# Three edits in the order of a hybrid encoder layer: the norm's VectorE steps bound to their written place, the splits of the heads' output spread over more of the GLU stage, and channel sums ten taps later

## Chip, cores and metric

The kernel runs on one core of one Trainium2 chip. The metric is the device time of one execution in microseconds. Three runs of the kernel before took 2465.12, 2465.72 and 2464.33 us, median 2465.12 us. The engines are called as the profile calls them: PE (TensorE, matmuls) and PEld (its weight loads), DVE (VectorE), ACT (ScalarE), POOL (GpSimd), SP (SyncE, which here only issues DMAs).

## The reference, cut to what matters

One layer for a sequence of 512 frames with 2048 channels, in float32:

```python
h = rmsnorm(x, g_pre)
qkv, z_a, b_raw, a_raw, glu_in, z_b, gate_logits = split(h @ w_in)
# A: gated DeltaNet, 16 heads of 128
o_a = gated_delta_chunked(q, k, v, g_log, beta)
o_a = rmsnorm(o_a, g_dn_out) * silu(z_a)
y_a = o_a @ w_br_a
# B: Conformer convolution
u = glu(glu_in)
u = causal_depthwise_conv(u, w_dw) + b_dw          # 31 taps
u = silu(layernorm(u, ln_g, ln_b)) * silu(z_b)     # over the 2048 channels
y_b = u @ w_br_b
mixed = (gate_a * y_a + gate_b * y_b) @ w_out
x = x + rmsnorm(mixed, g_post)
x = x + rmsnorm(sigmoid(x @ w_ple_gate) * (p @ w_ple_proj), g_ple)
```

The change touches the depthwise convolution, the layernorm and what turns `o_a` into operands of the product with `w_br_a`.

## The kernel before

**Products.** Channels or frames lie on the 128 partitions, tiles are 128x512 float32. Every product of two float32 matrices is made of three matmuls: each operand is split into a high part (a cast on ACT) and a low part (a subtraction on DVE or POOL), and high by high, high by low and low by high are added up in PSUM. Weights come in pieces: SP loads a raw tile of two pieces (L122), ACT casts the high part (L127), and DVE or POOL subtracts the low part (L128, by `low_part[0]`). A piece serves 12 matmuls. The ring of split pieces has four buffers (`ring`), so that one is in use and up to three stand ready.

**Stages.** After the input norm come the gate products with a Strassen-like scheme, then the heads (48 tiles of q, k, v and the chunked recurrence), then the GLU tiles, branch A (`o_a @ w_br_a`, L1076), branch B (`u @ w_br_b`, the same function), the output product and the embedding product. The part of this case runs from the GLU tiles to the start of branch B.

**GLU and convolution.** `glu_pair(i)` (L991) gives channel tile i: two tiles of 48 matmuls each, the first ends in a sigmoid on ACT (L911), the second in a product on DVE (L981). For i above 11 each pair is followed by one job of branch A of 48 matmuls (`next_ya`). `convs` (L938) does the 31 taps of a tile on DVE, one instruction for each tap (L954), bound to its written place; from the GLU stage on it reads a copy of the tile in PSUM (`up`). Two tiles are done beside it by `side_convs` (L964): ACT makes a product for a tap (L972) and POOL adds it (L973). A finished tile is written to DRAM (L961) and added to a running sum over channels on POOL by `filtered` (L915: L918 for the first tile, L920 for the others); for DVE's tiles this is called at tap 18 of the next tile. Tiles of the convolutions come from the pool `s2` with 17 buffers.

**Splits of the heads' output.** `split_oa` (L1064) takes the 16 heads' tiles one by one: ACT casts the high part (L1067), POOL subtracts the low part (L1069, bound). It is started after GLU pair 9 with a period of 15 ticks and finished by force after pair 11. The 32 tiles lie in the pool `lop` (23 buffers) and, from head 11's low part on, in `s2`.

**Norm.** `layer_norm` (L1134) loads the filtered tiles again as each is done (L1139, SP), takes the mean from a product of the channel sum with ones (L1143, L1145), subtracts it from each tile (L1150, DVE), squares the tile on ACT (L1152), and adds the squares up (L1154, DVE). Four small products give the variance (L1158), POOL takes the power -0.5 (L1162), a product with ones spreads it into PSUM (L1170). Then for each tile: multiply (L1174, DVE), SiLU (L1175, ACT), multiply with the other gate (L1179, DVE), high part (L1181, ACT), low part (L1183, DVE). These are the operands uT of branch B. Branch A has four column blocks j of 192 matmuls; at the end of a block four DVE instructions (L1102) empty its four PSUM banks, which the next block uses.

**What sets the order.** The code is written as generators. `tick` is called after every matmul of these stages and advances each active generator when its period, or the number that it yielded last, has run out: this gives the written order. Then a scheduler orders each engine's queue: it runs the program on a model of the engines and gives an engine, whenever that is free, the instruction that comes first in the written order among those that are ready, so that an instruction that is ready early moves ahead of earlier ones that are not. Buffers of a pool are given out in written order. `pin` (`keep_in_program_order`, L104) takes this freedom away on one side: the instruction is placed behind the one written last before it on the same engine. Later unbound instructions may still move ahead of it. On the chip each queue is then worked off in that order.

Of the kernel before, what the change touches and what calls it, by code (L numbers as in the profile page):

```python
# [12 lines left out]
ALU = mybir.AluOpType  # L13
# [68 lines left out]
def _body(ctx, tc, A, out):  # L82
    nc = tc.nc
# [20 lines left out]
    pin = tc.keep_in_program_order  # L104
# [4 lines left out]
    def vv(col, n=1):  # L109
        return vec[:, col:col + n]  # L110
# [28 lines left out]
    jobs = deque()  # L139
    active = []  # L140

    def spawn(gen, period, key=None):
        active.append([gen, period, period, key])
# [11 lines left out]
    def finish(key=None):  # L155
        while any(key is None or a[3] == key for a in active):
            for a in list(active):
                if (key is None or a[3] == key) and next(a[0], "end") == "end":
                    active.remove(a)
# [755 lines left out]
    def filtered(i, y):  # L915
        if not acc:
            acc.append(slots.tile([P, T], F32, tag="s", name="acc"))
            nc.gpsimd.tensor_copy(acc[0], y)  # L918
        else:
            nc.gpsimd.tensor_tensor(acc[0], acc[0], y, ALU.add)  # L920
        done.add(i)

    def near(held=True):
        if not waiting or len(taken) == NK:
            return None
        i, u = waiting.popleft()
        taken.add(i)
        if ups and held:
            up = ups.tile([P, T], F32, tag="u", name="up")
            nc.scalar.copy(up, u)  # L930
            u = up
        y = cpool[0].tile([P, T], F32, tag=cpool[1], name="uc")
        nc.scalar.activation(y, u, AF.Identity, scale=vv(V_DW + i * TAPS + TAPS - 1), bias=vv(V_BDW + i))
        return i, u, y

    def pace(s):
        return (3 + s % 2) if ups else CP

    def convs():
        ready = last = None  # L940
        while scanning[0] < NH // 2 - 1:
            yield 4
        while len(done) < NK:
            ready = ready or near()
            if not ready:
                if last and len(taken) == NK:
                    filtered(*last)
                    last = None
                yield 1
                continue  # L950
            (i, u, y), ready = ready, None
            w0 = V_DW + i * TAPS
            for s in range(1, TAPS):
                pin(nc.vector.scalar_tensor_tensor(y[:, s:], u[:, 0:T - s], vv(w0 + TAPS - 1 - s), y[:, s:], ALU.mult, ALU.add))  # L954
                if s == 18 and last:
                    filtered(*last)
                    last = None
                if s == 24:
                    ready = near()
                yield pace(s)  # L960
            nc.sync.dma_start(u_dram[i], y)  # L961
            last = i, y
# [28 lines left out]
    def glu_pair(i):  # L991
        glu_b(i)
        glu_a(i)
# [48 lines left out]
    gate_b = [[None] * 4 for _ in range(NTT)]  # L1042

    jobs.append(lambda: spawn(convs(), CP, "convs"))
    for i in range(2, 5):
        glu_pair(i)
# [13 lines left out]
    def low(n, name, dt=F32R):  # L1060
        return lop.tile([P, T], dt, tag="lop", name=name) if n < LOP else s2.tile([P, T], dt, tag="s2", name=name)
    oT = []

    def split_oa():  # L1064
        for h in range(NH):
            oh = low(2 * h, "oh")
            nc.scalar.copy(oh, o_a[h])  # L1067
            ol = low(2 * h + 1, "ol")
            pin(nc.gpsimd.tensor_tensor(ol, o_a[h], oh.bitcast(F32), ALU.subtract))  # L1069
            oT.append((oh, ol))  # L1070
            yield
# [39 lines left out]
    def next_ya():  # L1111
        j, q = ya.pop(0)
        if q == 1:
            jobs.append(lambda: load_gate(j))
        branch(A["w_br_a"], j, q, oT, evac_ya)

    for i in range(5, NK):
        glu_pair(i)
        if i == 9:
            jobs.append(lambda: spawn(split_oa(), 15, "oa"))  # L1120
        if i == 11:
            jobs.append(lambda: finish("oa"))
        if i > 11:
            next_ya()
# [6 lines left out]
    def hp(name):  # L1131
        return hpool.tile([P, T], F32, tag="h", name=name)

    def layer_norm():  # L1134
        for i in range(NK):
            while i not in done:
                yield
            u_t[i] = hp("ur")
            nc.sync.dma_start(u_t[i], u_dram[i])  # L1139
            yield 1  # L1140
        low_part[0] = nc.vector
        pm = ups.tile([P, T], F32, tag="u", name="sum_ps")
        mm(pm, ones, acc[0], start=True, stop=True)  # L1143
        mean = ups.tile([P, T], F32, tag="u", name="mean_ps")
        nc.scalar.activation(mean, pm, AF.Copy, scale=1.0 / D)  # L1145
        acc2 = hp("acc2")
        yield 6
        for i in range(NK):
            u = u_t[i]
            nc.vector.tensor_tensor(u, u, mean, ALU.subtract)  # L1150
            sq = hp("lsq") if i else acc2
            nc.scalar.activation(sq, u, AF.Square)  # L1152
            if i:
                nc.vector.tensor_tensor(acc2, acc2, sq, ALU.add)  # L1154
            yield 7
        pvr = ups.tile([P, T], F32, tag="u", name="var_ps")
        for tt in range(NTT):
            mm(pvr[:, tt:tt + 1], acc2[:, tt * P:(tt + 1) * P], ones[:, 0:1], start=True, stop=True)  # L1158
        var = lnp.tile([P, NTT], F32, name="var")
        nc.vector.tensor_scalar(var, pvr[:, 0:NTT], 1.0 / D, EPS, ALU.mult, ALU.add)  # L1160
        rst = lnp.tile([P, NTT], F32, name="rst")
        nc.gpsimd.tensor_tensor(rst, var, mhalf_c[:, 0:NTT], ALU.pow)  # L1162
        dg = hp("dg")
        for tt in range(NTT):
            nc.vector.tensor_scalar(dg[:, tt * P:(tt + 1) * P], ident, rst[:, tt:tt + 1], None, ALU.mult)
        for i in range(3):
            load_zb(i)
        yield 12
        rstd = ups.tile([P, T], F32, tag="u", name="rstd_ps")
        mm(rstd, ones, dg, start=True, stop=True)  # L1170
        yield 6
        for i in range(NK):
            u = u_t[i]
            nc.vector.tensor_tensor(u, u, rstd, ALU.mult)  # L1174
            nc.scalar.activation(u, u, AF.Silu, scale=vv(V_LNG + i), bias=vv(V_LNB + i))  # L1175
            yield 6
            if i + 3 < NK:
                load_zb(i + 3)
            nc.vector.tensor_tensor(u, u, zb[i], ALU.mult)  # L1179
            uh = low(0, "uh")  # L1180
            nc.scalar.copy(uh, u)  # L1181
            ul = low(LOP if i < 33 - LOP else 0, "ul")
            nc.vector.tensor_tensor(ul, u, uh.bitcast(F32), ALU.subtract)  # L1183
            uT[i] = (uh, ul)
            yield 6

    def load_zb(i):
        zb[i] = hp("zb")
        nc.sync.dma_start(zb[i], zb_dram[i])

    norm = layer_norm()
    jobs.append(lambda: spawn(norm, 4, "norm"))
    while ya:
# [121 lines left out]
    def bcast_row(src, j, home=S3_):  # L1315
        t = unit(home, "grow")
        nc.scalar.dma_start(t, src[:, j * T:(j + 1) * T].broadcast_to([P, T]))
        return t
# [261 lines left out]
    def ple_last(gp):  # L1580
        def f(tt, ps):
            e = e_t4[tt][3]
            sg = slots.tile([P, T], F32, tag="s", name="fsg")
            for h in range(2):
                c = slice(h * 256, h * 256 + 256)
                nc.scalar.activation(sg[:, c], ps[:, c], AF.Sigmoid)
                nc.vector.tensor_tensor(e[:, c], sg[:, c], e[:, c], ALU.mult)
                junk = slots.tile([P, T], F32, tag="s", name="fjunk")
                nc.scalar.activation(junk[:, c], e[:, c], AF.Square, accum_out=ssp[:, tt, 3 + h:4 + h])
            nc.vector.tensor_tensor(sg, e, gp, ALU.mult)  # L1590
            e_t4[tt][3] = sg
        return f
# [24 lines left out]
    last = ple_last(bcast_row(A["g_ple"], 3))  # L1617
    for k in range(12, NK):
        hold(k)
    for tt in range(NTT):  # L1620
# [9 lines left out]
        for j in range(4):  # L1630
            s = e_t4[tt][j]
# [67 lines left out]
```

## Time and profile before

| | |
|---|---|
| profiled execution | 2464.67 us, its span 2462.9 us, granted clock 0.995 |
| PE busy | 2418.6 us, 98% of the span |
| DVE busy | 1787.0 us, 73% |
| ACT busy | 1207.6 us, 49% |
| POOL busy | 507.3 us, 21% |
| GLU stage beside the convolutions | about 1490 to 1775 us |
| norm (L1143 to the last L1183) | 1852 to 1924 us |
| branch B begins | 1931.7 us |

A row of the order in time has the start in us, the time in us, engine, line, operation, output and inputs, shapes and count; a bracket at its end is the idle time of the engine before it and what ended it. Rows of a stretch have the busy us of PE, PEld, DVE, ACT and POOL with the number of instructions, then the granted clock of PE (1.00 is full), the share of DMA and GB/s. Rows of groups give busy us and mean ns, then the idle time before them. Rows of waits give the total, the number and the longest.

### The profile page before, as it was taken

The numbers are of one execution on the slowest core, as the hardware profiler recorded it, in microseconds if no ns is written. First come the engines' busy times: TensorE is split into PE (matmuls) and PEld (weight loads), VectorE is DVE, ScalarE is ACT, GpSimd is POOL, SyncE is SP. The second block draws the span as 40 slices with busy tenths as digits, with TensorE's granted clock in tenths as the row PEclk, the third lists the DMA queues.
The fourth block names the chain that finished last, engine by engine and source line by source line (L and its number), as shares of the span: only waits on it lengthen the run. The fifth ranks groups of instructions, "written<-read, shape, count | busy, mean of one in ns | idle before, by whom it ended". The sixth has DMA issues, their size and how long they took to land.

```text
span 2462.9 us, 33750 instructions
## 1 busy us (share of the span) xinstructions
PE 2418.6 (98%) x11962; PEld 1989.9 (81%) x11962; DVE 1787.0 (73%) x3345; ACT 1207.6 (49%) x2357; POOL 507.3 (21%) x531
## 2 busy tenths in 40 slices
PE   8999999999999999999999998999998999999998
PEld 7888888887888888888888887877886888788886
DVE  7878878777677676777767678987998454667644
ACT  6455545554655555455655644444325333554532
POOL 0001110013212112132200007898630000000000
PEclk9999999999999999999999999999998999999999
DMA  7567776666636353466622222343534432665542
GB/s 269 172 199 187 218 196 203 196 175 198 187 108 184 101 161 124 138 185 170 181 79 90 73 86 90 112 145 105 173 114 144 132 129 93 226 216 174 194 171 77
DMA packets 145289, 380.21 MB, mean 154 GB/s; under 512 B 16352, under 2 KB 24800, under 8 KB 145120
## 3 DMA queue, kind: packets, MB, share of 16 engines
q1 hardware_dynamic: 119008, 319.32, 39.2%
q0 software_dynamic: 23808, 54.54, 10.3%
q10 hardware_dynamic: 2304, 4.20, 0.5%
q8 instruction: 94, 1.54, 0.3%
q14 instruction: 75, 0.61, 0.1%
HBM read 329.75 MB, written 48.23 MB: 153 GB/s over the span
## 4 chain that ended last, share of the span: by engine, by line
PE 90%; POOL 3%; issue 2%; DVE 2%; ACT 1%; DMA 1%; SPq 0%; POOLq 0%; DVEq 0%; ACTq 0%
PE g L186 13%; PE g L188 13%; PE g L184 13%; PE zp L422 6%; PE zp L421 6%; PE zp L423 6%; PE yp L1092 4%; PE yp L1094 4%; PE yp L1090 4%; PE f L1382 2%; PE f L1383 2%; PE f L1384 2%; PE f L1550 2%; PE f L1548 2%; PE f L1549 2%
## 5 line engine op out<-in xcount | busy, mean ns | idle before, releaser
L188 PE MATMUL g<-hh,w 128*128 128x512 f32 x1536 | 612.0, 398 | 9.1 <-POOL w L128 9.1
L186 PE MATMUL g<-hl,w 128*128 128x512 f32 x1536 | 612.2, 399 | 0.0
L184 PE MATMUL g<-hh,w 128*128 128x512 f32 x1536 | 610.6, 398 | 0.5 <-ACT w L127 0.5
L127 ACT CAST w<-raw 128x512 fp32r<-128x512 f32 x588 | 357.7, 618 | 472.5 <-PE yp L1094 184.4
L128 DVE TENSOR_TENSOR w<-raw,w 128x512 fp32r<-128x512 f32 x464 | 318.8, 694 | 190.2 <-ACT w L127 187.8
L188 PEld LDWEIGHTS g<-hh,w 128*128 128x128 f32 x1536 | 290.2, 189 | 67.8 <-POOL w L128 11.7
L186 PEld LDWEIGHTS g<-hl,w 128*128 128x128 f32 x1536 | 290.0, 189 | 55.9 <-issue 1.4
L184 PEld LDWEIGHTS g<-hh,w 128*128 128x128 f32 x1536 | 290.2, 189 | 54.4 <-ACT w L127 0.9
L954 DVE SCALAR_TENSOR_TENSOR uc<-up,vec,uc 128x506 f32<-128x506 f32 (+29 forms) x390 | 284.0, 734 | 11.9
L128 POOL TENSOR_TENSOR w<-raw,w 128x512 fp32r<-128x512 f32 x124 | 161.8, 1314 | 141.8 <-DVE uc L954 74.5
L656 DVE SCALAR_TENSOR_TENSOR cv<-g,vec,cv 128x511 f32<-128x511 f32 x144 | 106.4, 739 | 28.2 <-ACT cv L654 27.6
L1092 PE MATMUL yp<-w,oh 128*128 128x512 f32 x256 | 101.5, 397 | 10.3 <-DVE w L128 9.0
L1094 PE MATMUL yp<-w,ol 128*128 128x512 f32 x256 | 100.6, 394 | 0.0
L1090 PE MATMUL yp<-w,oh 128*128 128x512 f32 x256 | 100.4, 396 | 0.0
L1090 PE MATMUL yp<-w,uh 128*128 128x512 f32 x256 | 100.2, 392 | 0.0
L1094 PE MATMUL yp<-w,ul 128*128 128x512 f32 x256 | 100.2, 393 | 0.0
L1092 PE MATMUL yp<-w,uh 128*128 128x512 f32 x256 | 100.2, 391 | 0.0
L842 DVE TENSOR_TENSOR prod<-UT,VT 128x2 f32<-128x2 f32 (+30 forms) x248 | 87.8, 354 | 6.5
L1006 POOL DMA_DIRECT2D wsum<-in_w_out x96 | 75.4, 837 | 71.1 <-DMA wsum<-in_w_out 37.1
L1326 POOL TENSOR_TENSOR rmsm<-totm,mhalf_c 128x2 f32<-128x2 f32 x2 | 1.4, 698 | 399.5 <-DVE totm L1324 399.5
L973 POOL TENSOR_TENSOR uc<-uc,pr 128x511 f32<-128x511 f32 (+29 forms) x60 | 77.9, 1298 | 3.5 <-ACT pr L972 2.5
L1382 PE MATMUL f<-wsp,oph 128*128 128x512 f32 x192 | 75.6, 394 | 1.7 <-ACT wsp L1363 1.7
(386 smaller groups left out, 4958.4 us busy)
## 6 DMA issues: line engine op xcount, KB each, us to landing
raw<-in_w_in SPq DMA_DIRECT2D x194, 512.0 KB, 3.4
wsum<-in_w_out POOLq DMA_DIRECT2D x96, 256.0 KB, 5.6
raw<-in_w_ple_gate SPq DMA_DIRECT2D x40, 512.0 KB, 3.4
wo_sums<-wsum POOLq DMA_DIRECT2D x64, 256.0 KB, 4.1
raw<-in_w_br_a SPq DMA_DIRECT2D x32, 512.0 KB, 3.4
raw<-in_w_br_b SPq DMA_DIRECT2D x32, 512.0 KB, 3.3
raw<-in_w_ga SPq DMA_DIRECT2D x24, 512.0 KB, 4.5
raw<-in_w_gb SPq DMA_DIRECT2D x24, 512.0 KB, 4.8
```

Source lines behind the costliest of these rows:

```text
L127: nc.scalar.copy(hi, rq)
L128: low_part[0].tensor_tensor(lo, rq, hi.bitcast(F32), ALU.subtract)
L184: mm(ps, wh, rh, start=(k == 0), stop=False)
L186: mm(ps, wh, rl, start=False, stop=False)
L188: mm(ps, wl, rh, start=False, stop=(k == NK - 1))
L421: mm(ps[pr][t], lh, wh, start=q + n == 0, stop=False)
L422: mm(ps[pr][t], ll, wh, start=False, stop=False)
L423: mm(ps[pr][t], lh, wl, start=False, stop=q == 3 and n == 1)
L954: pin(nc.vector.scalar_tensor_tensor(y[:, s:], u[:, 0:T - s], vv(w0 + TAPS - 1 - s), y[:, s:], ALU.mult, ALU.add))
L1090: mm(ps[tt], lh[:, b], wh, start=k == 0, stop=False)
L1092: mm(ps[tt], lh[:, b], wl, start=False, stop=False)
L1094: mm(ps[tt], ll[:, b], wh, start=False, stop=k == NK - 1)
```

## The change

Three edits, with no instruction added or removed:

- In `convs`, `filtered` of the tile before is called at tap 28 instead of tap 18.
- `split_oa` is started after GLU pair 5 with a period of 40 ticks, instead of after pair 9 with 15. The forced finish after pair 11 stays.
- In `layer_norm`, the subtraction of the mean (L1150), the addition of the squares (L1154) and the multiplication by the inverse deviation (L1174) are bound with `pin`.

```diff
@@ convs
-                if s == 18 and last:
+                if s == 28 and last:
                     filtered(*last)
                     last = None
                 if s == 24:
@@ the GLU loop
     for i in range(5, NK):
         glu_pair(i)
-        if i == 9:
-            jobs.append(lambda: spawn(split_oa(), 15, "oa"))
+        if i == 5:
+            jobs.append(lambda: spawn(split_oa(), 40, "oa"))
         if i == 11:
             jobs.append(lambda: finish("oa"))
@@ layer_norm
-            nc.vector.tensor_tensor(u, u, mean, ALU.subtract)
+            pin(nc.vector.tensor_tensor(u, u, mean, ALU.subtract))
             sq = hp("lsq") if i else acc2
             nc.scalar.activation(sq, u, AF.Square)
             if i:
-                nc.vector.tensor_tensor(acc2, acc2, sq, ALU.add)
+                pin(nc.vector.tensor_tensor(acc2, acc2, sq, ALU.add))
             yield 7
...
-            nc.vector.tensor_tensor(u, u, rstd, ALU.mult)
+            pin(nc.vector.tensor_tensor(u, u, rstd, ALU.mult))
             nc.scalar.activation(u, u, AF.Silu, scale=vv(V_LNG + i), bias=vv(V_LNB + i))
```

## The prediction

> **What bounds the kernel now.** I read the page first, then who waited for whom on TensorE, then the busy times in stretches of 20 us over the part that the change touches, and last the instructions in order of time there.
>
> ```profile
> PE 2418.6 (98%) x11962; PEld 1989.9 (81%) x11962; DVE 1787.0 (73%) x3345; ACT 1207.6 (49%) x2357; POOL 507.3 (21%) x531
> ```
> ```profile
> PE g L188 <- POOL w L128: 9.1, 6, 3.5
> PE yp L1092 <- DVE w L128: 9.0, 1, 9.0
> ```
> TensorE is the bound, so only time in which it stands or runs slowly can be won. Its two longest waits (total, times, longest) are both for a weight split, line 128: on POOL while the GLU tiles run, on DVE once in branch A. The undisturbed pace is read from 27 steps between two matmuls:
>
> ```profile
> 1925.62 0.39 PE L1090 MATMUL yp<-w,oh 128*128 128x512 f32 x1
> ...
> 1931.74 0.39 PE L1090 MATMUL yp<-w,uh 128*128 128x512 f32 x1
> ```
> 6.12/27 = 0.2267 us each; a piece of weights (12 matmuls) lasts 2.72 us, and the ring holds three pieces ahead, 8.2 us.
>
> ```profile
> 1560.00:1580.00 20.00, 20.00 (x90) 16.58 (x89) 19.54 (x30) 9.45 (x16) 16.04 (x14) 1.00 0.33 110
> 1620.00:1640.00 20.00, 18.79 (x81) 14.89 (x81) 17.85 (x26) 8.94 (x16) 20.00 (x17) 1.00 0.45 145
> 1640.00:1660.00 20.00, 15.78 (x61) 12.24 (x60) 16.23 (x23) 6.14 (x11) 20.00 (x17) 0.91 0.33 106
> 1660.00:1680.00 20.00, 19.12 (x83) 15.14 (x81) 12.00 (x18) 9.53 (x16) 17.17 (x15) 1.00 0.37 118
> 1680.00:1700.00 20.00, 19.35 (x85) 16.02 (x86) 19.11 (x27) 9.24 (x17) 16.51 (x14) 1.00 0.38 119
> 1860.00:1880.00 20.00, 10.98 (x36) 8.14 (x34) 16.68 (x31) 8.70 (x14) 1.01 (x1) 0.69 0.27 82
> ```
> Columns: busy us of PE, PEld, DVE, ACT, POOL, then the granted clock. A full stretch has 90 matmuls. From 1620 to 1700 matmuls are missing while POOL is full, and at 1860 over half are missing and the clock falls to 0.69. What each hole costs comes from time stamps that TensorE itself set:
>
> ```profile
> 1599.73 0.69 DVE L981 TENSOR_TENSOR sg<-g,sg 128x512 f32<-128x512 f32 x1 [0.29 <-PE g L188]
> ...
> 1708.07 0.69 DVE L981 TENSOR_TENSOR sg<-g,sg 128x512 f32<-128x512 f32 x1 [3.77 <-PE g L188]
> ...
> 1825.64 0.69 DVE L1102 TENSOR_TENSOR gt<-yp,gt 128x512 f32<-128x512 f32 x1 [1.78 <-PE yp L1094]
> ```
> The two L981 rows are the ends of GLU pairs 9 and 13. Between them lie four pairs of 96 matmuls and one branch job of 48: 432 x 0.2267 = 97.9 us. They took 108.3, so **10.4 us** are lost. The L1102 row marks the last-but-nine matmul of column block 1 of branch A, so block 2 begins near 1827.5; branch B begins at 1931.74. Two blocks are 384 x 0.2267 = 87.0 us and took 104.3: 17.2 more. The norm's own products stay, below put at 2.9, so **14.3 us** could be won.
>
> **The channel sum (18 to 28).** It moves 16 POOL steps of 1.3 us (L918, L920) ten taps down in the code, thereby letting the norm's loads of u (SP's queue, L1139) be written later for all but the last tile, whose place is unchanged.
>
> ```profile
> 1517.40 0.61 POOL L918 COPY acc<-uc 128x512 f32<-128x512 f32 x1 [7.44 <-DVE uc L954]
> ...
> 1541.35 1.30 POOL L920 TENSOR_TENSOR acc<-acc,uc 128x512 f32<-128x512 f32 x1 [1.10 <-DVE uc L954]
> ...
> 1602.82 1.31 POOL L1069 TENSOR_TENSOR ol<-oa,oh 128x512 fp32r<-128x512 f32 x1
> ...
> 1655.23 2.53 POOL L1069 TENSOR_TENSOR ol<-oa,oh 128x512 fp32r<-128x512 f32 x2
> ```
> Already now the sum stands right where the last tap of its own tile ends (it waits for that tap), not 18 taps, some 14 us, later. It isn't bound, so the scheduler puts it where POOL is free; a later line changes only its rank. I cost it at 0. Bounds: a gain of 5 if L918's 7.44 us wait, behind which a split makes TensorE stand 3.5 us, did go; a loss of 2 if a late sum frees its buffer late. The sum of the terms takes 0, since the row shows the step ahead of its place.
>
> **The heads' splits (from after pair 9 every 15 ticks, to after pair 5 every 40).** Nothing is added; 16 POOL steps (L1069) and their ACT casts move; no DMA among them.
>
> ```profile
> L128 POOL TENSOR_TENSOR w<-raw,w 128x512 fp32r<-128x512 f32 x124 | 161.8, 1314 | 141.8 <-DVE uc L954 74.5 <-ACT w L127 65.5 <-issue 1.4
> L973 POOL TENSOR_TENSOR uc<-uc,pr 128x511 f32<-128x511 f32 (+29 forms) x60 | 77.9, 1298 | 3.5 <-ACT pr L972 2.5
> L1069 POOL TENSOR_TENSOR ol<-oa,oh 128x512 fp32r<-128x512 f32 x16 | 20.6, 1304 | 0.0
> L1175 ACT ACTIVATE ur<-ur,vec 128x512 f32<-128x512 f32 x16 | 12.3, 809 | 3.9 <-DVE ur L1174 3.9
> L1181 ACT CAST uh<-ur 128x512 fp32r<-128x512 f32 x16 | 9.3, 618 | 3.9 <-DVE ur L1179 2.1 <-PE yp L1092 1.9
> ```
> Without L1069 a pair (96 ticks, 21.8 us) gives POOL 8 weight splits, 96/18 = 5.3 side-tap sums and about 0.9 channel sums, 14.2 x 1.27 = 18.0 us, 83%; the stretch at 1560 shows 16.04 of 20. (1.27 is a pair of L1069 at 1655, 2.53, halved.) At 15 ticks L1069 adds 6.4 x 1.27 = 8.1: 120% for 54 us, more than 8.2 us of ring can carry, hence the hole. At 40 ticks it adds 2.4 x 1.27 = 3.0: 97%. The generator runs 14 steps in pairs 6 to 11 (576 ticks), and the forced finish gives the last two at once, 2.5 us, which the ring carries. What can be left is the other cause in the same stretch, buffers:
>
> ```profile
> 1647.90 0.78 ACT L933 ACTIVATE uc<-up,vec 128x512 f32<-128x512 f32 x1 [3.33 <-POOL acc L920]
> ...
> 1660.27 0.72 ACT L972 ACTIVATE pr<-sg,vec 128x502 f32<-128x502 f32 x1 [7.92 <-POOL uc L973]
> ```
> From head 11 on the splits take nine tiles of the pool s2, and ACT, its casts for the weights behind it, waits until POOL frees one. This comes about one pair sooner now. With 3% to spare I leave 3.0 of the 10.4 us (bounds 0, as in the stretch at 1560, and 10.4, all of it moved): **gain 7.4**.
>
> **The norm's bound steps (L1150, L1154, L1174).** No instruction is added. Now:
>
> ```profile
> 1844.70 0.68 DVE L128 TENSOR_TENSOR w<-raw,w 128x512 fp32r<-128x512 f32 x1
> ...
> 1850.20 0.68 DVE L128 TENSOR_TENSOR w<-raw,w 128x512 fp32r<-128x512 f32 x1
> 1853.85 2.48 DVE L1150 TENSOR_TENSOR ur<-ur,mean_ps 128x512 f32<-128x512 f32 x4 [2.97 <-ACT mean_ps L1145]
> ...
> 1858.05 0.69 DVE L1150 TENSOR_TENSOR ur<-ur,mean_ps 128x512 f32<-128x512 f32 x1
> ...
> 1871.25 0.69 DVE L128 TENSOR_TENSOR w<-raw,w 128x512 fp32r<-128x512 f32 x1
> ...
> 1873.05 0.69 DVE L1154 TENSOR_TENSOR acc<-acc,lsq 128x512 f32<-128x512 f32 x1
> ...
> 1880.61 3.08 DVE L1174 TENSOR_TENSOR ur<-ur,rstd_ps 128x512 f32<-128x512 f32 x5 [1.60 <-PE rstd_ps L1170]
> ```
> ```profile
> 1844.00 0.62 ACT L127 CAST w<-raw 128x512 fp32r<-128x512 f32 x1 [2.10 <-PE yp L1094]
> ...
> 1853.98 0.62 ACT L127 CAST w<-raw 128x512 fp32r<-128x512 f32 x1 [0.17 <-PE yp L1094]
> ...
> 1858.77 0.63 ACT L1152 ACTIVATE lsq<-ur 128x512 f32<-128x512 f32 x1 [0.57 <-DVE ur L1150]
> ```
> ```profile
> 1861.90 1.07 PE L1090 MATMUL yp<-w,oh 128*128 128x512 f32 x4
> 1871.99 0.79 PE L1092 MATMUL yp<-w,oh 128*128 128x512 f32 x1 [9.02 <-DVE w L128]
> ...
> 1873.87 1.80 PE L1158 MATMUL var_ps<-cst,acc 128*128 128x1 f32 x8
> ...
> 1878.66 1.91 PE L1170 MATMUL rstd_ps<-dg,cst 128*128 128x512 f32 x2
> ...
> 1881.17 0.39 PE L1094 MATMUL yp<-w,ol 128*128 128x512 f32 x1
> ```
> From 1853.85 DVE runs subtractions of all 16 tiles ahead of their squares, and a weight split whose cast was done at 1854.6 waits until 1871.25. TensorE stands 9.0 us and then runs slowly to 1881.17. (Its own products at full pace: half of 1.80 and of 1.91, and 1.0 for the sum: 2.9.) Bound, subtraction i+1 stands behind addition i, which waits for ACT's square: 0.72 from subtraction to square (1858.05, 1858.77), 0.63, 0.08 back (cast 1844.00 + 0.62, split 1844.70), 0.60 for the addition (steps at 1871.25 to 1873.05): 2.03 us a tile, of which DVE is free 0.8. A ready split fits that gap; TensorE needs 2.03/2.72 = 0.75 splits a tile. So the stop goes. What is queued behind the waiting addition are splits and L1102; the scheduler puts ready ones ahead of it.
>
> Next late is the chain. It takes 0.6 + 15 x 2.03 = 31 us instead of 20; then as now about 7 us to the first L1174 (1873.74 to 1880.61); then 0.72 + 0.81 + 0.08 + 0.72 + 0.62 + 0.08 + 0.60 = 3.63 us a tile, 58 for 16: the last uT 97 us after the start. Branch B's first pass wants it 77.9 - 14.3 + 2.5 + 15 x 2.72 = 107 us after. These 10 us cover it; beyond them each microsecond counts fully. Uncovered are two handovers of four PSUM banks inside the chains (end of blocks 2 and 3): four L1102 in gaps 2 us apart need 8 us where TensorE wants them in 2.0; other ready matmuls fill in most. I leave 2.5 (bounds 0 and 14.3): **gain 11.8**.
>
> For the slow spell the rows give 9.2 us, from 1871.99 to 1881.17, where 13 matmuls and the two products at full pace take 4.8: 4.4 us extra. The Trainium skill ("TensorE: Matmul & The Clock Gate", "Part 1: The HAM clock gate") says about 3.4 us of sustained work restore the full clock, half of it lost. By that only 1.7 us would be extra and the forecast 2.7 later; the trace disagrees, perhaps as the norm's products break the work up, and I go by the rows.
>
> **Sum.** 7.4 + 11.8 = 19.2. The profiled execution took 2464.67 (span 2462.9): 2445.5. The median of the runs is 0.45 higher: **2446 us**.
>
> **Rivals.** (a) Buffers, not POOL's load, make the GLU hole: spreading only moves it. For it: the two ACT waits above; against it: POOL is full for 40 us just then. Only 11.8 is won: 2453. The Trainium skill ("Perfetto Trace Analysis", "Optimization Strategy") reads a recurring gap as a sign of too few buffers for the next tile; by that rule this is the case, and the trace bears it out in part. (b) The norm hole is only moved, to the bank handovers and to branch B waiting for uT: 7.4 and little more, 2456. (c) Nothing measurable: both holes reappear elsewhere, 2463. (d) Slower: the first chain is laid out with hardly a split in its gaps. Then DVE hands out the next one after 31.1 us instead of 17.4, and TensorE stands 9.0 + 13.7 - 2.72m for m splits inside; it is worse than now for m under 5. At m = 0, with 7.4 won before, 13.7 - 7.4 = 6.3 late: 2471. Against it: a cast done at 1854.6 offers a split at once. That the change doesn't do what it says holds only for the channel sum.
>
> **Chances.** Forecast 0.60, (a) 0.14, (b) 0.11, (c) 0.08, (d) 0.07. Faster by over 0.2% (4.9 us, about what a measurement of this kernel can tell): 0.85; within: 0.08; slower: 0.07. The range goes from both residues at zero (24.7 won, 2440) to (b) with a microsecond, 2457, leaving out (c) and (d).
>
> **What would show it.** The stretches from 1620 to 1700 at about 90 matmuls with POOL near 19 of 20 from 1525 on; no 9 us wait at L1092; splits between subtraction and addition; tiles of the norm 2 us, then 3.6 us apart; POOL's L918 still waiting. A wait for uT in branch B, or for L1102, or POOL waits before 1620 would prove me wrong.

## The result and the profile after

The changed kernel takes **2446.77 us** (median of 4 runs, 2446.04 to 2447.55) against 2464.72 us for the kernel before, timed beside it (median of 4, 2462.76 to 2465.72): a ratio of **0.9928, 95% interval 0.9911 to 0.9945**. Timed again in five rounds it took 2445.68 us, ratio 0.9921 (0.9907 to 0.9935). The profiled execution took 2447.55 us, its span 2445.8. The forecast was 2446.

First who waited for whom on TensorE between 1460 and 1960 us, in the profile after (total, times, longest):

```profile
PE g L188 <- POOL w L128: 4.1, 2, 3.5
...
PE rstd_ps L1170 <- DVE dg L1165: 0.8, 1, 0.8
PE yp L1090 <- DVE gt L1102: 0.7, 1, 0.7
```

The 9.0 us wait of L1092 for DVE's split is gone, and of the six waits of L188 two are left, 4.1 us instead of 9.1. A wait for L1102, one of the signs that the prediction named against itself, does show, but it is 0.7 us long. The stretches of 20 us in the profile after (busy us of PE, PEld, DVE, ACT, POOL, then the granted clock):

```profile
1520.00:1540.00 20.00, 18.71 (x71) 15.25 (x72) 19.15 (x28) 7.83 (x13) 19.92 (x17) 0.83 0.52 169
...
1620.00:1640.00 20.00, 19.97 (x89) 16.21 (x88) 17.85 (x26) 8.73 (x16) 20.00 (x16) 1.00 0.38 122
1640.00:1660.00 20.00, 20.00 (x90) 16.57 (x89) 17.66 (x25) 8.66 (x15) 18.51 (x16) 1.00 0.33 107
...
1860.00:1880.00 20.00, 20.00 (x94) 16.43 (x92) 17.33 (x29) 10.48 (x17) 0.89 (x1) 1.00 0.40 131
```

Where 61 matmuls stood at 1640 there are 90, and where 36 stood at 1860 there are 94; small products of the norm are among them, 10 of the 36 and 8 of the 94. POOL has 19.5 us or more of each 20 from 1520 to 1580, where it had 19.0, 17.0 and 16.0 before: the spreading moved its steps forward. The hole that is left lies at 1520, with 71 matmuls, and in the stretch before it, with 79; before the change these two had 84 and 72. The time stamps that gave the two holes their size, in order of time, after:

```profile
1602.76 0.69 DVE L981 TENSOR_TENSOR sg<-g,sg 128x512 f32<-128x512 f32 x1 [0.52 <-PE g L188]
...
1702.20 0.69 DVE L981 TENSOR_TENSOR sg<-g,sg 128x512 f32<-128x512 f32 x1 [3.34 <-PE g L188]
...
1819.77 0.69 DVE L1102 TENSOR_TENSOR gt<-yp,gt 128x512 f32<-128x512 f32 x1 [1.77 <-PE yp L1094]
```
```profile
1914.18 0.47 PE L1090 MATMUL yp<-w,uh 128*128 128x512 f32 x1 [0.66 <-DVE gt L1102]
```

GLU pairs 9 to 13 take 99.44 us instead of 108.34, so 8.90 are won, and 1.5 over the 97.9 of undisturbed work are left. From the end of column block 1 to branch B it is 94.41 instead of 106.10: 11.69 won. Between pair 13 and that block both profiles have the same 117.57. The account: 8.90 + 11.69 = 20.6 are won. Against that, the way to POOL's L918 took 2.0 us more in this execution (1519.40 against 1517.40), the way from there to pair 9 took 1.0 more (83.36 against 82.33), and what follows the start of branch B took 0.5 more. This leaves 17.1, the difference of the two spans.

The norm's chain in the profile after, DVE in order of time, a tile of the first stage and one of the second:

```profile
1851.78 0.68 DVE L1150 TENSOR_TENSOR ur<-ur,mean_ps 128x512 f32<-128x512 f32 x1
1852.38 0.69 DVE L128 TENSOR_TENSOR w<-raw,w 128x512 fp32r<-128x512 f32 x1
1853.16 0.69 DVE L1154 TENSOR_TENSOR acc<-acc,lsq 128x512 f32<-128x512 f32 x1
...
1890.99 0.68 DVE L1174 TENSOR_TENSOR ur<-ur,rstd_ps 128x512 f32<-128x512 f32 x1
1892.56 0.69 DVE L1179 TENSOR_TENSOR ur<-ur,zb 128x512 f32<-128x512 f32 x1 [0.88 <-ACT ur L1175]
1893.16 0.68 DVE L128 TENSOR_TENSOR w<-raw,w 128x512 fp32r<-128x512 f32 x1
1893.94 0.69 DVE L1183 TENSOR_TENSOR ul<-ur,uh 128x512 fp32r<-128x512 f32 x1
1894.55 0.68 DVE L1174 TENSOR_TENSOR ur<-ur,rstd_ps 128x512 f32<-128x512 f32 x1
...
1942.99 0.68 DVE L1183 TENSOR_TENSOR ul<-ur,uh 128x512 fp32r<-128x512 f32 x1
```

A weight split stands in the gap in which the chain waits for ACT's square: 0.60 from L1150 to the split, 0.78 to L1154. In the second stage L1174 returns after 3.56 us here, after 3.84 in the mean of all tiles. The last low part ends at 1943.7; branch B needs it at 1914.18 + 15 x 2.72 = 1955, and no wait for it shows.

### The profile page after: what moved, and what is told of

It reads as the page before. It is cut to its first block, busy times and chain, and to the rows that moved or that the text cites. A ratio compares the mean times of both kernels' runs of the same rounds, so it can differ in the third digit from the quotient of the medians.

```text
span 2445.8 us, 33732 instructions
## 1 busy us (share of the span) xinstructions
PE 2414.0 (99%) x11962; PEld 1985.5 (81%) x11962; DVE 1792.4 (73%) x3345; ACT 1208.8 (49%) x2357; POOL 507.0 (21%) x531
## 4 chain that ended last, share of the span: by engine, by line
PE 89%; DVE 3%; POOL 2%; DMA 2%; issue 2%; ACT 2%; SPq 0%; POOLq 0%; DVEq 0%; ACTq 0%
PE g L186 13%; PE g L188 13%; PE g L184 13%; PE zp L423 6%; PE zp L421 6%; PE zp L422 5%; PE yp L1090 4%; PE yp L1094 4%; PE yp L1092 4%; PE f L1382 2%; PE f L1383 2%; PE f L1384 2%; PE f L1548 2%; PE f L1549 2%; PE f L1550 2%
## 5 line engine op out<-in xcount | busy, mean ns | idle before, releaser
L188 PE MATMUL g<-hh,w 128*128 128x512 f32 x1536 | 610.6, 397 | 4.1 <-POOL w L128 4.1
L128 DVE TENSOR_TENSOR w<-raw,w 128x512 fp32r<-128x512 f32 x464 | 321.5, 700 | 169.2 <-ACT w L127 166.6
L188 PEld LDWEIGHTS g<-hh,w 128*128 128x128 f32 x1536 | 289.8, 189 | 61.5 <-POOL w L128 5.4
L954 DVE SCALAR_TENSOR_TENSOR uc<-up,vec,uc 128x506 f32<-128x506 f32 (+29 forms) x390 | 284.0, 734 | 11.9
L128 POOL TENSOR_TENSOR w<-raw,w 128x512 fp32r<-128x512 f32 x124 | 161.4, 1314 | 136.7 <-DVE uc L954 74.5
L1092 PE MATMUL yp<-w,uh 128*128 128x512 f32 x256 | 100.0, 391 | 0.0
L1092 PE MATMUL yp<-w,oh 128*128 128x512 f32 x256 | 99.6, 389 | 0.0
```

The lines of the kernel that those rows point to most:

```text
L128: low_part[0].tensor_tensor(lo, rq, hi.bitcast(F32), ALU.subtract)
L188: mm(ps, wl, rh, start=False, stop=(k == NK - 1))
L1092: mm(ps[tt], lh[:, b], wl, start=False, stop=False)
```

## Experiments

**One part alone: the binding of the norm's three steps**, put into the kernel before.

```diff
-            nc.vector.tensor_tensor(u, u, mean, ALU.subtract)
+            pin(nc.vector.tensor_tensor(u, u, mean, ALU.subtract))
...
-                nc.vector.tensor_tensor(acc2, acc2, sq, ALU.add)
+                pin(nc.vector.tensor_tensor(acc2, acc2, sq, ALU.add))
...
-            nc.vector.tensor_tensor(u, u, rstd, ALU.mult)
+            pin(nc.vector.tensor_tensor(u, u, rstd, ALU.mult))
```

> The kernel before with only the norm's three VectorE steps (L1150, L1154, L1174) bound to their written place. Theory (the norm hole is won by the binding alone, by itself 11.7 us between the comparison of the two traces' L1102 and first uh product): 2464.7 - 11.7 = about 2453 us, TensorE's 9 us wait at L1092 gone, the GLU stop of about 9 us at pairs 12 and 13 still there. Rival (the norm hole is only moved, because branch B's first products then wait for uT): 2460 to 2465 us.

2455.07 us against 2465.04 (ratio 0.9962, 0.9949 to 0.9974): 10.0 won, 1.7 less than expected. TensorE's wait and one stretch of this kernel:

```profile
PE g L188 <- POOL w L128: 10.2, 7, 3.4
```
```profile
1640.00:1660.00 20.00, 15.75 (x69) 12.37 (x68) 16.26 (x23) 7.19 (x13) 20.00 (x18) 1.00 0.37 121
```

The GLU hole is untouched, the 9 us wait gone; from the end of block 1 to branch B its trace has 94.61 us (1827.83 to 1922.44), nearly as in the kernel after (94.41). The norm hole is won by the binding alone, not moved.

**One part alone: the splits of the heads' output spread**, put into the kernel before.

```diff
-        if i == 9:
-            jobs.append(lambda: spawn(split_oa(), 15, "oa"))
+        if i == 5:
+            jobs.append(lambda: spawn(split_oa(), 40, "oa"))
```

> The kernel before with only the splits of the heads' output begun at pair 5 in 40 ticks. Theory (GpSimd's load of splits and channel-sum steps together makes the GLU stop): the stop goes, 2464.7 - 8 = 2456 to 2458 us, GpSimd at 19 us or more of each 20 from 1540 to 1600. Rival (the stop is made by the place where buffers come free): no change, 2463 to 2466 us. The norm hole stays in both.

2458.11 us (ratio 0.9972, 0.9960 to 0.9983): 6.9 won. Pairs 9 to 13 take 98.94 us (1601.00 to 1699.94). TensorE's waits of this kernel, and the stretch that was worst before:

```profile
PE yp L1092 <- DVE w L128: 9.0, 1, 9.0
PE g L188 <- POOL w L128: 3.5, 1, 3.5
```
```profile
1640.00:1660.00 20.00, 20.00 (x90) 16.57 (x89) 17.64 (x26) 8.84 (x15) 18.58 (x16) 1.00 0.27 96
```

The two parts alone win 10.0 + 6.9 = 16.9 of the 18.0 by medians. For the buffers, ACT's waits for a free tile (pr) between 1520 and 1700, first of the kernel before, then of this one:

```profile
ACT pr L972 <- POOL uc L973: 24.6, 8, 7.9
```
```profile
ACT pr L972 <- POOL uc L973: 25.1, 10, 5.0
```

ACT waits for tiles as long as before, and TensorE doesn't feel it. The number of buffers itself was not varied. But the kernel before shows that a late ACT did not make the hole: had its casts come too late, POOL would have stood and waited for them. After this wait POOL waits for ACT only at 1661.58 again, 1.34 us:

```profile
1600.39 1.30 POOL L128 TENSOR_TENSOR w<-raw,w 128x512 fp32r<-128x512 f32 x1 [1.43 <-ACT w L127]
```

In between POOL works without a break, and the two stops of TensorE in the hole that are over 1 us (ending at 1646.68 and 1655.34) lie there. POOL had more to do than time.

**One part alone: the channel sum at tap 28**, put into the kernel before.

```diff
-                if s == 18 and last:
+                if s == 28 and last:
```

> The kernel before with only the channel sums written ten taps later. Theory (the sums are not bound to the place where they are written, so hardly an instruction moves): 2464 us, within 1 us of before. Rival (the later place takes the wait of 7.4 us at L918 away): about 2460 us.

2465.26 us, ratio 1.0004 (0.9995 to 1.0012). This edit does nothing that can be measured (the interval allows 1 us won to 3 lost): L918 still waits, 8.21 us here.

**Less time for the splits**: the kernel after, with their start after pair 7 and 24 ticks.

```diff
-        if i == 5:
-            jobs.append(lambda: spawn(split_oa(), 40, "oa"))
+        if i == 7:
+            jobs.append(lambda: spawn(split_oa(), 24, "oa"))
```

> The kernel after with the splits of the heads' output begun after pair 7 in 24 ticks instead of after pair 5 in 40. Theory (GpSimd's load decides, and a load a few per cent over its time is paid out of the ring's stock of ready weights): 2446.8 + 0 to 2 us, GpSimd at 20 of 20 us from 1590 to 1650, no stop over 3 us at L188 there. Rival (a late start by itself makes the stop, whatever the load): + 4 us or more, the waits at L188 in pairs 11 to 13 back.

2447.23 us, ratio 0.9925 (0.9912 to 0.9938): the same as after. Two stretches of it and TensorE's wait:

```profile
1600.00:1620.00 20.00, 20.00 (x90) 16.58 (x89) 19.15 (x27) 12.67 (x22) 19.92 (x17) 1.00 0.52 175
1620.00:1640.00 20.00, 17.79 (x77) 14.10 (x77) 17.85 (x26) 6.57 (x12) 20.00 (x17) 1.00 0.35 115
```
```profile
PE g L188 <- POOL w L128: 6.3, 4, 3.5
```

POOL is full and two small waits come back; pairs 9 to 13 take 101.96 us, 2.5 more than after, of which the medians show 0.5 to 1.5. A load of a few per cent over the time is paid for the most part out of the three pieces that stand ready. Where the load ceases to be free was not searched for.

**Only the subtraction bound**: the kernel after without the binding of L1154 and L1174.

```diff
-                pin(nc.vector.tensor_tensor(acc2, acc2, sq, ALU.add))
+                nc.vector.tensor_tensor(acc2, acc2, sq, ALU.add)
...
-            pin(nc.vector.tensor_tensor(u, u, rstd, ALU.mult))
+            nc.vector.tensor_tensor(u, u, rstd, ALU.mult)
```

> The kernel after with only the norm's subtraction (L1150) bound; the addition (L1154) and the product with rstd (L1174) float again. Theory (in the second stage the chain's steps go ahead of the weight splits again, about 28 VectorE steps before the next split, so TensorE stops for several us at the start of that stage): 2446.8 + 5 to 9 = 2452 to 2456 us, the wait at L1092 or L1090 on VectorE's w back with 5 us or more. Rival (only the first stage's binding matters, and a shorter second stage helps): 2446 us or below.

2454.99 us, ratio 0.9956 (0.9944 to 0.9968): 8.2 slower than after. TensorE's wait, and DVE in order of time at the start of the second stage:

```profile
PE yp L1092 <- DVE w L128: 7.2, 1, 7.2
```
```profile
1878.74 0.68 DVE L128 TENSOR_TENSOR w<-raw,w 128x512 fp32r<-128x512 f32 x1
1880.04 3.08 DVE L1174 TENSOR_TENSOR ur<-ur,rstd_ps 128x512 f32<-128x512 f32 x5 [0.62 <-PE rstd_ps L1170]
1883.04 1.89 DVE L1179 TENSOR_TENSOR ur<-ur,zb 128x512 f32<-128x512 f32 x3
...
1896.92 0.69 DVE L128 TENSOR_TENSOR w<-raw,w 128x512 fp32r<-128x512 f32 x1
```

Between the two splits lie 18.2 us of chain steps. So a chain that is only bound in the first stage rebuilds the stop in the second. With L1150 bound, the binding of L1174 is worth 8 to 9 us. L1154 stood in the same place with and without its binding, so that part of the edit changes nothing.

**The weight splits bound too**: the kernel after, with DVE's L128 bound from the norm's first product to the end of the first stage.

```diff
+    in_norm = []
...
-            low_part[0].tensor_tensor(lo, rq, hi.bitcast(F32), ALU.subtract)
+            w_lo = low_part[0].tensor_tensor(lo, rq, hi.bitcast(F32), ALU.subtract)
+            if in_norm:
+                pin(w_lo)
...
+        in_norm.append(1)
...
+        in_norm.clear()
```

> The kernel after with VectorE's weight splits (L128) in the first stage of the norm bound to their written place too, so that they can no longer go ahead into the gaps of the chain. Theory (the binding helps because splits that are free to go ahead fill the chain's gaps): TensorE stops for the first stage's 30 us less its stock, 2446.8 + 25 to 45 = 2472 to 2492 us. Rival (holding the chain's steps back is all that matters): 2446 to 2449 us.

2470.80 us, ratio 1.0021 (1.0012 to 1.0030): 24 slower than after. The stretches of this kernel:

```profile
1820.00:1840.00 20.00, 13.56 (x60) 10.89 (x58) 18.69 (x27) 3.11 (x5) 2.92 (x3) 0.94 0.15 51
1840.00:1860.00 20.00, 15.19 (x50) 10.91 (x50) 11.43 (x18) 7.58 (x13) 0.77 (x1) 0.72 0.23 79
1860.00:1880.00 20.00, 13.12 (x51) 10.19 (x50) 14.86 (x24) 7.72 (x13) 0.00 (x0) 0.91 0.24 80
```

Against 90, 84 and 94 matmuls in the same stretches after, 107 are missing. The way from the end of block 1 to branch B, 94.41 us in after, takes 117.11 here (1819.77 to 1936.88): 22.7 lost. The direction is the theory's and the size just below its lower end. But the chain's gaps are not all of it. TensorE in order of time (L128 is L129 here, L1143 is L1147):

```profile
1832.49 1.07 PE L1093 MATMUL yp<-w,oh 128*128 128x512 f32 x4
1840.83 2.07 PE L1147 MATMUL sum_ps<-acc,cst 128*128 128x512 f32 x2 [7.27 <-POOL acc L923]
1846.88 0.79 PE L1095 MATMUL yp<-w,oh 128*128 128x512 f32 x1 [3.98 <-DVE w L129]
```

From 1824.11 on DVE does the last 20 taps of the convolution without one split between them, where after has seven, and its next split is at 1846.14, behind the chain's first addition. The bound splits, written behind the taps, can no longer go ahead of these either. The stop up to 1846.88 and the slow matmuls behind it cost about 14 us, what follows in the chain's gaps the other 9. What makes the change good is thus a pair: the chain's steps are held, and the splits stay free to go ahead, into the chain's gaps and between the taps before it.

**A longer second stage**: two steps more in each tile of the kernel after, which leave the values as they are.

```diff
             nc.scalar.activation(u, u, AF.Silu, scale=vv(V_LNG + i), bias=vv(V_LNB + i))
+            nc.vector.tensor_scalar(u, u, 1.0, None, ALU.mult)
+            nc.scalar.copy(u, u)
```

> The kernel after with one VectorE step (times 1.0) and one ScalarE copy more in each tile of the norm's second stage, which leave the values as they are: about 1.5 us more a tile, 24 us in all. Theory (the last uT has some 11 us in hand before branch B wants it; what is over is lost): 2446.8 + 10 to 14 = about 2459 us, with waits of the first uh products on uT. Rival one (the chain has no cover, its length is paid in full): + 24 us. Rival two (branch B does not wait for the chain): + 2 us or less.

2451.60 us, ratio 0.9942 (0.9929 to 0.9956): 4.8 slower than after. TensorE's wait in this kernel:

```profile
PE yp L1090 <- ACT uh L1183: 4.9, 3, 1.6
```

L1183 is L1181 two lines further on: branch B waits for the last three high parts. The size expected, 10 to 14 us, was missed because the added steps were shorter: they lengthen a tile by 1.1 us (0.46 for the product, 0.65 for the copy), not 1.5. The last uh starts at 1959.5, its low part 17 us later than in after, not 24. 17 less the 4.9 that were lost is a cover of 12 us, near the 11 that the profile after shows (1943.7 to 1955); the prediction had put 10.

**The channel sum bound to tap 28**: the kernel after, so that the third edit does what its line says.

```diff
-            nc.gpsimd.tensor_copy(acc[0], y)
+            pin(nc.gpsimd.tensor_copy(acc[0], y))
...
-            nc.gpsimd.tensor_tensor(acc[0], acc[0], y, ALU.add)
+            pin(nc.gpsimd.tensor_tensor(acc[0], acc[0], y, ALU.add))
```

> The kernel after with both GpSimd steps of the channel sum (L918, L920) bound to their written place, tap 28. Theory (L918 still goes ahead to a place where the tile that it copies isn't done, and stands 7.4 us on GpSimd with the splits behind it; TensorE then stops 3.5 us at L188 and runs slowly after it): that wait and that stop go, 2446.8 - 4 to 5 = about 2442 us. Rival (the splits behind L918 have slack, and the stop comes from another row): 2446 to 2448 us.

2450.87 us, ratio 0.9944 (0.9931 to 0.9958). Both views were wrong: the kernel got no faster, by its median 4 to 5 us slower than after (the intervals overlap). TensorE's longest wait of this kernel:

```profile
PE g L184 <- DVE sg L981: 8.7, 1, 8.7
```

POOL's wait and the 3.5 us stop at L188 are gone, as meant, and a longer stop stands in their place, for DVE. DVE in order of time, in after and then in this kernel:

```profile
1499.09 20.25 DVE L954 SCALAR_TENSOR_TENSOR uc<-sg,vec,uc 128x498 f32<-128x498 f32 x17
```
```profile
1499.33 26.63 DVE L954 SCALAR_TENSOR_TENSOR uc<-sg,vec,uc 128x497 f32<-128x497 f32 x16
```

These are the last taps of the first tile, the only one that is read from SBUF (sg) and not from PSUM (up). Line L954 in after, first 1499 to 1511.9 us, where POOL works, then 1512 to 1519.2, where it stands at L918 (duration in ns, least, median, most):

```profile
L954 DVE SCALAR_TENSOR_TENSOR uc<-sg,vec,uc x9: 1636/1644/1659, 1497.4 to 1510.9; 128x499 f32<-128x499 f32 x1, 128x498 f32<-128x498 f32 x1, 128x497 f32<-128x497 f32 x1, 128x496 f32<-128x496 f32 x1
```
```profile
L954 DVE SCALAR_TENSOR_TENSOR uc<-sg,vec,uc x10: 720/726/1642, 1510.9 to 1518.6; 128x491 f32<-128x491 f32 x1, 128x490 f32<-128x490 f32 x1, 128x489 f32<-128x489 f32 x1, 128x488 f32<-128x488 f32 x1
```

A tap takes 1.64 us beside POOL's steps and 0.73 while POOL stands. The wait at L918 was the time in which DVE caught up: without it each tap goes on at 1.64, and the GLU product behind them (L981) is late. The new theory: on operands in SBUF the two engines hold each other up, and nothing is won at L918 while the first tile reads SBUF.

**The first tile's taps from PSUM**: the kernel after, in which that tile too is copied to PSUM as soon as the pool for it is open. The tap (L954) and what stands behind it stand five lines further on.

```diff
+            in_ps = bool(ups)
             for s in range(1, TAPS):
+                if ups and not in_ps:
+                    up = ups.tile([P, T], F32, tag="u", name="up")
+                    nc.scalar.copy(up, u)
+                    u, in_ps = up, True
```

> The kernel after with the first tile of branch A's taps (those of L954 that read sg in SBUF) copied to PSUM as soon as there is room, as the later tiles are (lines behind L953 stand four or five further on). Theory (VectorE's taps that have all operands in SBUF and GpSimd's steps hold each other up: 1.64 us a tap beside GpSimd's steps against 0.72 us while GpSimd waits, and 0.73 us for taps out of PSUM beside GpSimd): the first tile's last 17 taps take about 13 us instead of 20, GpSimd's steps beside them 1.27 us instead of 1.70, the wait of 7.4 us at the first channel-sum step and TensorE's stop of 3.5 us with the slow products after it go (11 products missing in 1500 to 1520 and 19 in 1520 to 1540, by 0.226 us, 6.8 us): 2446.8 - 6.8 = about 2440 us. Rival one (the taps are slow for another reason, such as their place in the run): taps of 1.6 us out of PSUM too, 2446 to 2448 us. Rival two (what is won there is lost later in the stage, since GpSimd has no time left from 1540 on): taps of 0.73 us and 2444 to 2447 us.

**2440.48 us**, ratio 0.9900 (0.9885 to 0.9915), 5 to 6 us faster than after by the medians, where 6.8 was worked out. POOL's groups between 1497 and 1518 us (busy us, mean ns), in after and then in this kernel:

```profile
L128 POOL TENSOR_TENSOR w<-raw,w 128x512 fp32r<-128x512 f32 x5 | 8.6, 1728 | 0.0
L973 POOL TENSOR_TENSOR uc<-uc,pr 128x510 f32<-128x510 f32 (+3 forms) x4 | 6.6, 1658 | 0.2
```
```profile
L128 POOL TENSOR_TENSOR w<-raw,w 128x512 fp32r<-128x512 f32 x8 | 10.4, 1295 | 3.2 <-ACT w L127 3.2
L978 POOL TENSOR_TENSOR uc<-uc,pr 128x510 f32<-128x510 f32 (+5 forms) x6 | 7.7, 1288 | 0.2
```

And the first stretches of this kernel with its taps:

```profile
1500.00:1520.00 20.00, 20.00 (x90) 16.57 (x89) 18.51 (x27) 9.56 (x17) 17.35 (x15) 1.00 0.43 144
1520.00:1540.00 20.00, 20.00 (x90) 16.57 (x89) 17.97 (x25) 10.06 (x17) 18.66 (x16) 1.00 0.43 137
```
```profile
1494.12 14.52 DVE L959 SCALAR_TENSOR_TENSOR uc<-up,vec,uc 128x502 f32<-128x502 f32 x19
```

19 taps take 14.5 us where 21 took 25.2 in after (from 1494.17 on), POOL's steps fall from 1.7 to 1.29 us, and TensorE has its 90 matmuls at once. Both engines gain, which one engine's slowness would not explain.

**The same with the channel sum bound.**

```diff
+            pin(nc.gpsimd.tensor_copy(acc[0], y))
...
+            pin(nc.gpsimd.tensor_tensor(acc[0], acc[0], y, ALU.add))
```

> As the run before, with both GpSimd steps of the channel sum bound to their written place too. Theory: with the taps out of PSUM nothing stands at the first channel-sum step any more, so binding changes little: within 2 us of the run before, about 2440 us, and unlike the run with the binding alone no wait of TensorE on VectorE's sg. Rival (binding the sum by itself costs 4 us, whatever the taps read): 2444 us or more.

2439.33 us, ratio 0.9898 (0.9882 to 0.9915): not to be told from the run before. With the taps out of PSUM the binding costs nothing and wins nothing that can be measured, so the place of the sum by itself is not the matter. These two are the fastest versions found; their intervals meet that of after only at the ends.

The kernel after once more, as the measure for these runs, with nothing edited:

> The kernel after, unchanged, timed once more in five rounds, as the measure for the runs that start from it. Theory: 2447 us, ratio to before 0.993 with a narrower interval, so that the runs with the channel sum bound (2451 us) and with the first tile's taps out of PSUM (2440 us) stand outside it on either side. Rival: their differences of 4 and 6 us are the chips', and the ratio comes out at or above 0.9944 or at or below 0.990.

2445.68 us, as given above. The medians of both runs stand outside its interval; their intervals overlap it at an end, so that the case rests on the traces as much as on the times.

## Why the prediction was right

- **Which holes, and how much.** Two holes were to be won. GLU: 7.4 forecast, 8.9 in the trace, because the residue was 1.5 and not 3.0. Norm: 11.8 forecast, 11.7 in the trace. The sum of the terms, 19.2, came out as 20.6, and 3.5 of it were not seen in the total: 2.0 before the first L918, 1.0 just behind, 0.5 from branch B on. That the total came within 1 us of the forecast is thus in part luck, as two deviations went opposite ways. The 2.0 are not the change's: TensorE's 601st matmul is already 1.8 us later in after (140.08 against 138.31), more than 1300 us before the stage that the change touches. The 1.0 fits the slow matmuls after the stop at L918: they last 5.7 us in after and 3.5 in before, at half pace 1.1 us.
- **What is left of the norm's hole.** 2.5 were put for the handovers of the PSUM banks, and about 2.6 are left (from the start of block 2 to branch B 92.6 us, 1821.61 to 1914.18, over 87.0 + 2.9), but only the 0.7 of the wait for L1102 is a handover. TensorE's other waits there, 0.8 at L1170 and 0.6 at L1143, belong to the norm's own products. The size was right, its cause mostly another.
- **POOL's load as the cause of the GLU hole.** Shown by the spreading alone, which took the hole away, and by POOL's unbroken work in the hole before. Rival (a), by which spreading only moves the hole, falls: ACT's waits for buffers stayed at 25 us while the hole went. The Trainium skill ("Perfetto Trace Analysis", "Optimization Strategy") says that a recurring gap can mean too few buffers. Here it did not: the gap went with the number of buffers unchanged.
- **The norm's gaps.** Splits do stand between subtraction and addition, and a kernel whose splits can't go ahead is 24 us slower. That it took 2470.8 us, where rival (d) put 2471, is luck: (d) had no split in the chain and its whole loss there, and in that run ten stand between the first and the last addition, while more than half of the loss comes before. In after (d) does not happen because the splits stay free. Rival (b) falls with the norm's binding alone, which wins 10.0 us.
- **The cover of the chain.** Forecast 10 us, 11 in the profile after, 12 by the lengthened chain. The chain's parts were put at 31, 7 and 58 us and took 29.7, 4.5 and 61.4: the second stage is slower than forecast, since splits delay some of its tiles, and the way between the stages is shorter. The prediction's warning that beyond it each microsecond counts holds: of 17 added 4.9 were lost.
- **The slow spell after the stop.** Taken from the rows at 4.4 us. The gain of 11.7 needs it: the stop of 9.0 us and 1.7 for the slow spell would be 10.7 even with nothing left over. By the 1.7 that the Trainium skill ("TensorE: Matmul & The Clock Gate", "Part 1: The HAM clock gate") leads to, the norm would have given 9.1; the trace disagrees.
- **The channel sum at 0.** Borne out: 1.0004. (The edit moves 13 steps and not 16: the two tiles of `side_convs` and the last tile are added elsewhere.) But its upper bound, a gain of 5 if L918's wait went, was worked out wrongly: it took the wait as time that POOL loses, and did not ask what runs faster while POOL stands. With the wait gone and nothing else changed the kernel lost 4 to 5 us; the gain was there only when the taps were moved to PSUM as well.

## What to carry to other kernels

Before costing a wait as time to be won, look at what the other engines' instructions take during it: if they are twice as fast there, removing the wait moves the time. When a chain on one engine starves another, hold the chain back at its own place and leave the starved engine's suppliers free; binding both was worse here (2470.8 us) than binding neither (2458.1, the splits of the heads' output spread in both). A load is spread well when the stretches show the helper engine evenly just under full. By the prediction's way of counting, a start after pair 7 in 24 ticks asks for 106% of POOL's time for 87 us, which cost 2.5 us more than after; a fifth over for 54 us made the hole of 10.4.

## What the runs showed of the hardware

VectorE's taps and GpSimd's steps slow each other when both work on SBUF alone. Beside GpSimd's subtractions and additions a tap with both tensor inputs in SBUF takes 1.64 us, and 0.73 with GpSimd waiting. With one input in PSUM it takes 0.73 although GpSimd is busy for 17 of 20 us. GpSimd's step takes 1.7 us beside the first kind and 1.29 beside the last. The Trainium skill ("SBUF — State Buffer", "Who interferes with whom") says so: a VectorE instruction with two SBUF inputs contends with a GpSimd instruction that reads SBUF, and one with at most one SBUF input, outside the two-port modes, does not. The trace agrees on both halves.

After most of the stops of 3.4 to 9 us that these runs show, TensorE's matmuls run at about half pace for a while, whose length isn't fixed. In the profile after the first two slow ones are these:

```profile
1521.29 0.79 PE L188 MATMUL g<-hh,w 128*128 128x512 f32 x1 [3.45 <-POOL w L128]
1521.88 0.63 PE L184 MATMUL g<-hh,w 128*128 128x512 f32 x1
```

From there the steps are 0.43 us up to 1526.96, 5.7 us; after the same stop of 3.5 us it was 3.5 us in the kernel before and 3.0 in the kernel that starts the splits after pair 7, and 4.7 after the 8.7 us stop of the bound channel sum. Stops of 1.3 to 1.7 us were followed by full pace at once. A stop of 2.93 us went either way: in the kernel before, the one that ends at 1655.34 was followed by 4 us of mostly half pace; with the norm bound alone, the same stop, ending at 1657.53, by full pace.
